# Factor rows of the attention stage read back from DRAM in two DMAs of 64 rows each

## The chip, the cores and the metric

The kernel runs on one core of one Trainium2 chip. The metric is the device time of one execution in microseconds (us). Names of the engines, as the profile writes them: PE is the matrix engine, PEld its weight loads, DVE the vector engine, ACT the scalar engine, POOL the GpSimd engine, and SP the queue that issues most DMAs. A DMA is issued by a queue (SPq, ACTq, POOLq), runs on the core's DMA engines, and counts up a semaphore when its data has landed; whoever uses the data waits for that count.

## The reference

Two decoder layers over 1024 tokens of width 1024: a short convolution with a channel mixer, then sliding-window attention with a channel mixer. The change lies in the attention of the second layer:

```python
q = rmsnorm(q, q_gain)          # per head, 16 heads of 64
k = rmsnorm(k, k_gain)
scores = einsum(q, k) / sqrt(64) + alibi        # blocks of 128 queries, window of 128
p = softmax(concat([scores, sink]))[..., :-1]
out = einsum(p, v)
return out @ w_o
```

Two kinds of factors in it go through DRAM: the inverse root mean square of each query's head, by which q is multiplied, and the inverse of each softmax sum, by which out is multiplied.

## The kernel before

Activations lie with channels on the 128 partitions and the 1024 tokens along the row. Query tile i is 128 partitions by 1024 tokens and holds two heads, 64 partitions each; there are eight tiles. Products in float32 are made of three products of rounded parts (high and low), and the large projections use a scheme of seven half-size products in place of eight, for which sums of operands were written to DRAM (`q_ops`) and are streamed back.

The attention stage is a loop of steps (`step`, line 2456) in an order written out by hand; each engine runs its instructions in that order, and a queue likewise. A step works on one block b of 128 queries of one tile i, for eight blocks of eight tiles. Its parts: scores on PE (`scores`, L2276 and L2277), row maxima on DVE (`maxima`, L2291), exponents on ACT (L2311), the turn of the block on PE (L2319), its split on ACT and DVE (L2326, L2332), the product with the values on PE (L2345, L2346) and its collection (L2363, L2364). Between them stand pieces of the projection of later tiles (`three`, L2011), whose operands come by L2526 (`q_ops`, 512 KB each, into buffers XS and WH) and whose weights come by L1948 into WR. In the last two tiles the products of the output matrix take their place (L172, weights by L128). The scores of block n+1 use a bank that the maxima of block n release, so PE's scores wait for DVE's maxima.

A factor is made in columns, one token a partition, but is needed along the rows. For query tiles 2 to 7 (`keep_q`) and for the softmax sums of all but the last pair of tiles (`divide_steps`), the way is: `rows_to_dram` (line 1713) turns the columns on PE, copies them on ACT (L1718) and stores 8 KB from ACT's queue (L1719); a step or so later `rows_from_dram` (line 1721) is issued on SP and loads the factors back with each head's row repeated on its 64 partitions; 2.5 steps after that DVE multiplies (`rows_of`, L2199, for queries into `t["raw"]`; `scale`, L2393, for out). The multiplied q is then split by ACT (L2189) and POOL (L2194), and the next tile's scores use it.

The load for queries is 128 partitions by 1024 elements, 512 KB, and there are six (the profile shows `G<-rows_q` five times and `XS<-rows_q` once). The load for softmax sums is 128 by 512, 256 KB, and there are twelve (`s<-rows_d`). They go into `t["wide"]`, which is a tile G5 or G6 (XS7 for the last), and into tile s1, of which there is one.

Each DMA of SP and ACT takes one of eight counters (DMAHW0 to DMAHW7) in turn, so that an issue also waits for the DMA that had its counter before.

Of the kernel before, what the change touches and what calls it, by code (L numbers as in the profile page):

```python
# [19 lines left out]
NB = T // P  # L20
HD = 64
# [67 lines left out]
def trunk_kernel(ctx: ExitStack, tc: tile.TileContext, xT, small, w_in, w_out, w_q, w_v, w_o, w_gu, w_dn, out):  # L89
    nc = tc.nc  # L90
# [1569 lines left out]
    def attention_layer():  # L1660
# [59 lines left out]

        def rows_from_dram(out, src, c=slice(0, D)):

            rows = src.rearrange("(h b) c -> h (b c)", h=2)[:, c]
            n = rows.shape[1]
            nc.sync.dma_start(out, rows.unsqueeze(1).to_broadcast([2, HD, n]))

        it = {}
        v = []
# [410 lines left out]
        def keep_q(i, raw_of, side=None, later=0, steps=False):  # L2139
# [34 lines left out]
            def from_dram():  # L2174
                rows_from_dram(t["wide"], t["rows"])
# [190 lines left out]
        def divide_steps(p, h, k):  # L2366
# [35 lines left out]
            def fetch():  # L2402
                it["wide"] = slot("s1", (P, HALF))
                rows_from_dram(it["wide"], rows_dram[p, h], slice(k * HALF, (k + 1) * HALF))
# [13 lines left out]
        for p in range(NK // 2):  # L2418
            for h in (0, 1):
                for k in (0, 1):  # L2420
                    *steps, sink = divide_steps(p, h, k)
                    divisions[p, h, k] = wide, rows, scale = steps
                    n = 16 * p + 16 + 6 * h + 2 * k
# [198 lines left out]
        for e in (0, 1):  # L2622
            wide, rows, scale = divisions[NK // 2 - 1, 1, e]
# [117 lines left out]
```

## Time and profile before

| | us |
|---|---|
| median of three runs | 2006.52 |
| lowest, highest run | 2000.97, 2007.32 |
| profiled execution | 2003.35 |
| its span (first to last instruction) | 2001.6 |
| PE busy in the span | 1935.8 (97%) |
| DVE busy | 1335.0 (67%) |
| ACT busy | 897.4 (45%) |
| POOL busy | 294.4 (15%) |

The profile is one execution. Its steps begin where the attention stage does, near 1040 us, and the last turned block of it is near 1311 us. Lines of waits read "engine tile line <- who ended the wait: us in total, times, longest". Lines of a timeline read "start, duration, engine, line, operation, output <- input, shape, count", and a bracket gives the idle time of the engine before it and what ended that. A line of windows gives, for each stretch, its length, the busy time of each engine with the number of its instructions, PE's granted clock as a part of full speed, the mean busy share of the DMA engines, and GB/s. Waits on an engine that is not the bound cost nothing by themselves.

### The profile page before, as it was taken

Reading aid. Unit: us, or ns where it says so; the run is one execution under the profiler, and the core shown is the slowest. Engines: PE = TensorE matmul, PEld = TensorE weight load, DVE = VectorE, ACT = ScalarE, POOL = GpSimd, SP = SyncE. Lnnn points to the kernel's source line nnn. Section 1 sums busy time; section 2 is a strip of 40 time slices with the busy share of each in tenths; the row PEclk is TensorE's granted clock in tenths of the full one; section 3 lists DMA queues with packets and bytes.
Section 4 is the critical chain, followed back from the end, with each engine's and each line's share of the span. In section 5 each row is a group of like instructions: output and inputs, shape, how many; then the busy total and the mean of one; then the engine's idle time right before and its main releaser. Section 6 shows DMA issues by size and latency. Waiting matters only on the chain.

```text
span 2001.6 us, 25275 instructions
## 1 busy us (share of the span) xinstructions
PE 1935.8 (97%) x8961; PEld 1611.1 (80%) x8961; DVE 1335.0 (67%) x2293; ACT 897.4 (45%) x1765; POOL 294.4 (15%) x367
## 2 busy tenths in 40 slices
PE   9999999999999999999997767999999999999999
PEld 8888888888888888888986656788888888888887
DVE  8898777965565566657766646788766565566553
ACT  5543555433333344544565536655433333344441
POOL 0011221011121100100143225320011111100000
PEclk9999999999999999999998878999999999999999
DMA  8787594578887559954735542141565665467663
GB/s 319 253 231 183 123 253 122 179 218 254 239 206 212 149 187 357 285 192 137 263 132 175 172 135 79 54 170 58 204 169 184 194 174 183 133 223 272 212 218 105
DMA packets 157634, 380.51 MB, mean 190 GB/s; under 512 B 15620, under 2 KB 27204, under 8 KB 157508
## 3 DMA queue, kind: packets, MB, share of 16 engines
q1 hardware_dynamic: 121732, 269.45, 39.4%
q0 software_dynamic: 35248, 109.33, 22.2%
q8 instruction: 70, 1.15, 0.2%
q14 instruction: 56, 0.46, 0.1%
q10 hardware_dynamic: 528, 0.13, 0.0%
HBM read 307.18 MB, written 149.52 MB: 228 GB/s over the span
## 4 chain that ended last, share of the span: by engine, by line
PE 89%; DMA 5%; DVE 4%; issue 1%; ACT 1%; POOL 1%; ACTq 0%; POOLq 0%; SPq 0%; DVEq 0%
PE acc L1004 16%; PE acc L1005 16%; PE acc L1007 16%; PE P L1004 9%; PE P L1005 9%; PE P L1007 9%; DMA G<-rows_q 3%; PE acc L172 2%; PE P L2011 2%; PE P L1678 1%; PE acc L176 1%; PE acc L2011 1%; PE acc L1137 1%; PE acc L1139 1%; PE acc L1138 1%
## 5 line engine op out<-in xcount | busy, mean ns | idle before, releaser
L1004 PE MATMUL acc<-XS,G 128*128 128x512 f32 x926 | 360.4, 389 | 0.0
L1005 PE MATMUL acc<-XS,G 128*128 128x512 f32 x926 | 360.2, 389 | 0.0
L1007 PE MATMUL acc<-XS,G 128*128 128x512 f32 x926 | 360.2, 389 | 0.0
L1004 PE MATMUL P<-A,G 128*128 128x512 f32 x550 | 214.1, 389 | 0.0
L1007 PE MATMUL P<-A,G 128*128 128x512 f32 x550 | 214.0, 389 | 0.0
L1005 PE MATMUL P<-A,G 128*128 128x512 f32 x550 | 214.0, 389 | 0.0
L1004 PEld LDWEIGHTS acc<-XS,G 128*128 128x128 f32 x926 | 173.8, 188 | 36.2
L1007 PEld LDWEIGHTS acc<-XS,G 128*128 128x128 f32 x926 | 173.8, 188 | 36.1
L1005 PEld LDWEIGHTS acc<-XS,G 128*128 128x128 f32 x926 | 173.8, 188 | 36.0
L1004 PE MATMUL acc<-A,G 128*128 128x512 f32 x442 | 172.1, 389 | 0.0
L1007 PE MATMUL acc<-A,G 128*128 128x512 f32 x442 | 172.0, 389 | 0.0
L1005 PE MATMUL acc<-A,G 128*128 128x512 f32 x442 | 171.9, 389 | 0.0
L938 DVE TENSOR_TENSOR G<-WR,G 128x512 fp32r<-128x512 f32 (+1 forms) x216 | 144.3, 668 | 30.5 <-ACT G L937 30.2
L938 DVE TENSOR_TENSOR G<-WL,G 128x512 fp32r<-128x512 f32 x168 | 115.1, 685 | 73.4 <-ACT G L937 73.4
L937 ACT CAST G<-WR 128x512 fp32r<-128x512 f32 (+1 forms) x216 | 130.5, 605 | 64.2 <-PE acc L1007 26.5
L937 ACT CAST G<-WH 128x512 fp32r<-128x512 f32 (+1 forms) x174 | 104.7, 601 | 82.9 <-PE acc L1007 37.9
L938 DVE TENSOR_TENSOR G<-WH,G 128x512 fp32r<-128x512 f32 (+1 forms) x174 | 115.6, 665 | 19.6 <-ACT G L937 19.6
L1339 ACT ACTIVATE G<-G 128x512 f32<-128x512 f32 x88 | 55.8, 634 | 158.9 <-DVE G L1436 153.1
L1004 PEld LDWEIGHTS P<-A,G 128*128 128x128 f32 x550 | 103.2, 188 | 21.5
L1007 PEld LDWEIGHTS P<-A,G 128*128 128x128 f32 x550 | 103.2, 188 | 21.4
L1005 PEld LDWEIGHTS P<-A,G 128*128 128x128 f32 x550 | 103.2, 188 | 21.4
L937 ACT CAST G<-WL 128x512 fp32r<-128x512 f32 x168 | 103.4, 616 | 23.9 <-DVE WL L886 12.9
(420 smaller groups left out, 3798.7 us busy)
## 6 DMA issues: line engine op xcount, KB each, us to landing
G<-h SPq DMA_DIRECT2D x70, 512.0 KB, 6.1
s<-in_w_dn SPq DMA_DIRECT2D x32, 704.0 KB, 8.7
h<-X POOLq DMA_DIRECT2D x44, 512.0 KB, 5.3
s<-s POOLq DMA_DIRECT2D x32, 704.0 KB, 7.0
WR<-s SPq DMA_DIRECT2D x79, 256.0 KB, 3.1
WR<-in_w_gu SPq DMA_DIRECT2D x36, 512.0 KB, 3.2
WH<-in_w_gu SPq DMA_DIRECT2D x36, 512.0 KB, 3.1
XS<-q_ops SPq DMA_DIRECT2D x36, 512.0 KB, 7.4
```

The source lines that it names most:

```text
L172: pe.matmul(ps.half(h), wh, xs[:, j, c], start=first and j == 0, stop=False)
L176: pe.matmul(ps.half(h), wl, xs[:, 0, c], start=False, stop=last)
L937: lambda: act.copy(out_hi, raw),
L938: lambda: lo_eng.tensor_tensor(out_lo, raw, plain(out_hi), ALU.subtract),
L1004: pe.matmul(ps, w[:, 0, c], x[:, 0, :], start=start and e == 0, stop=False, skip_group_check=True)
L1005: pe.matmul(ps, w[:, 0, c], x[:, 1, :], start=False, stop=False, skip_group_check=True)
L1007: pe.matmul(ps, w[:, 1, c], x[:, 0, :], start=False, stop=last, skip_group_check=True)
L1137: pe.matmul(ps, hi[:, kc], xs[:, 0, c], start=k == 0, stop=False, skip_group_check=True)
L1138: pe.matmul(ps, hi[:, kc], xs[:, 1, c], start=False, stop=False, skip_group_check=True)
L1139: pe.matmul(ps, lo[:, kc], xs[:, 0, c], start=False, stop=k == n_op - 1, skip_group_check=True)
L1339: state["silu"] = act.activation(x, x, AF.Silu)
L2011: pe.matmul(ps, g[:, w, c], x[:, b, :], start=begin and i == 0, stop=end and i == 2, skip_group_check=True)
```

## The change

`rows_from_dram` issues two DMAs in place of one: head 0's row to partitions 0 to 63, then head 1's row to partitions 64 to 127. Bytes, the place in the order, and everything else are as before. All 18 loads change.

```diff
         def rows_from_dram(out, src, c=slice(0, D)):
 
-            rows = src.rearrange("(h b) c -> h (b c)", h=2)[:, c]
-            n = rows.shape[1]
-            nc.sync.dma_start(out, rows.unsqueeze(1).to_broadcast([2, HD, n]))
+            for h in (0, 1):
+                row = src[h * NB : (h + 1) * NB].rearrange("b c -> (b c)")[c]
+                nc.sync.dma_start(out[h * HD : (h + 1) * HD, :], row.unsqueeze(0).to_broadcast([HD, row.shape[0]]))
```

The source of the DMA before is described as 2 rows, each repeated 64 times, of n elements; each of the two DMAs after it is described as 64 repeats of n elements.

SP's queue has 726 entries after the change and 708 before. These are its rows around the first load of query factors, before and then after; in brackets are the counts that each waits for.

```order
L2526 DMA XS_1106_7534<-q_ops 128x2x512 [waits DMAHW6_49,PE_49]
L1725 DMA G_1241_8733<-rows_q_8839 128x1x1024 [waits DMAHW3_49,Activation_49]
L2526 DMA XS_1113_7572<-q_ops 128x2x512 [waits DMAHW7_49,PE_49]
L1948 DMA WR_7842<-s_104 128x512 [waits DMAHW0_49,Pool_49]
L1948 DMA WR_7842<-s_104 128x512 [waits DMAHW1_49,Pool_49]
```

```order
L2526 DMA XS_1106_7534<-q_ops 128x2x512 [waits DMAHW6_49,PE_49]
L1725 DMA G_1241_8733<-rows_q_8839 64x1024 [waits DMAHW3_49,Activation_49]
L1725 DMA G_1241_8733<-rows_q_8839 64x1024 [waits DMAHW7_49]
L2526 DMA XS_1113_7572<-q_ops 128x2x512 [waits DMAHW0_49,PE_49]
L1948 DMA WR_7842<-s_104 128x512 [waits DMAHW1_49,Pool_49]
L1948 DMA WR_7842<-s_104 128x512 [waits DMAHW2_49,Pool_49]
```

The second half took the place and the counter of the operand load behind it, and the loads behind it in these rows moved by one counter.

On DVE no row was added. These are its rows around the multiplication that uses that load (G_1241_8733), after the change and then before it.

```order
L2364 TENSOR_TENSOR G_1218_8569<-P_1269_8948,G_1218_8569 64x2x2x64 [waits Activation_49]
L2199 TENSOR_TENSOR G_1176_8270<-G_1176_8270,G_1241_8733 128x512 [waits DMAHW7_49,DMAHW6_49]
L2291 ISA G_1187_8368,mx_8596<-P_1270_8958,cst_61 128x192 [waits PE_49]
L2291 ISA mx_8596 128x1
L2291 ISA G_1187_8368,mx_8596<-P_1270_8958,cst_61 128x192
L2291 ISA mx_8596 128x1
L2199 TENSOR_TENSOR G_1176_8270<-G_1176_8270,G_1241_8733 128x512
```

```order
L2364 TENSOR_TENSOR G_1218_8569<-P_1269_8947,G_1218_8569 64x2x2x64 [waits Activation_49]
L2199 TENSOR_TENSOR G_1176_8270<-G_1176_8270,G_1241_8733 128x512 [waits DMAHW6_49]
L2291 ISA G_1187_8368,mx_8596<-P_1270_8957,cst_61 128x192 [waits PE_49]
L2291 ISA mx_8596 128x1
L2291 ISA G_1187_8368,mx_8596<-P_1270_8957,cst_61 128x192
```

The first multiplication waits for two counters in place of one; the row maxima (L2291) stand behind it on DVE as before.

## The prediction

> **What bounds the kernel now.** I read five views in this order: the page, the waits by engine in the attention stretch, the timeline and the windows there, and the chain that ended last. Of the page, the line of PE's busy tenths (40 slices of 50 us):
>
> ```profile
> PE   9999999999999999999997767999999999999999
> ```
>
> PE sets the pace of nearly the whole program. The exception is slices 22 to 25, from 1050 to 1250 us, where it is busy to 6 or 7 tenths. That is the attention stage, the only one that calls the changed function. The next view is who waited for whom from 1040 to 1330 us, the first row of PE's, then those of DVE on factor rows; the columns are total us, times, longest.
>
> ```profile
> PE P L2276 <- DVE mx L2291: 41.4, 14, 9.0
> ```
>
> ```profile
> DVE G L2199 <- DMA G<-rows_q: 21.9, 3, 9.5
> ...
> DVE WH L2199 <- DMA G<-rows_q: 15.9, 2, 7.9
> DVE G L2393 <- DMA s<-rows_d: 5.6, 2, 3.5
> ...
> DVE XS L2199 <- DMA XS<-rows_q: 3.8, 1, 3.8
> ```
>
> PE's scores (L2276) wait for DVE's row maxima, and DVE itself waits for the factor rows: 21.9 + 15.9 + 3.8 = 41.6 us for the six tiles of queries and 5.6 us for the denominators. The timeline of the first such stop shows issue, use, and PE's first matmul after it (start, duration, and in brackets the idle time before it and what ended it).
>
> ```profile
> 1067.54 0.61 SPq L1725 DMA_DIRECT2D G<-rows_q  x1
> 1081.68 0.69 DVE L2199 TENSOR_TENSOR G<-G,G 128x512 f32<-128x512 f32 x1 [8.52 <-DMA G<-rows_q]
> 1083.35 0.53 PE L2276 MATMUL P<-A,G 128*128 128x192 f32 x1 [8.09 <-DVE mx L2291]
> ```
>
> The load takes 14.1 us from issue to use. DVE was ready for it at 1081.68 - 8.52 = 1073.16, so it has 5.6 us of cover and is 8.5 us late. Why it takes so long is in the windows: one while only such a load runs, one of full traffic, and one of a whole period of 16 steps. The last three columns are PE's granted clock, the mean busy share of the DMA engines, and GB/s.
>
> ```profile
> 1197.00:1200.00 3.00, 0.00 (x0) 0.00 (x0) 0.00 (x0) 0.00 (x0) 0.00 (x0) 0.58 0.13 53
> 1062.04:1073.16 11.12, 10.58 (x68) 8.73 (x67) 10.16 (x34) 8.18 (x30) 3.02 (x4) 1.00 0.85 279
> 1062.04:1139.73 77.69, 55.91 (x305) 47.03 (x304) 45.38 (x127) 39.51 (x124) 20.82 (x19) 0.78 0.49 158
> ```
>
> Alone, the load keeps a share of 0.13 busy. The page averages over 16 engines, so that is two of them, 26 GB/s each. Under full traffic 0.85 x 16 = 13.6 engines carry 279 GB/s, 21 each. So each of the two engines runs as fast as any; there are just two. 512 KB at 53 GB/s is 9.9 us. The source of the load has an outer dimension of 2, the heads.
>
> A third thing: what is issued behind the load suffers too. This is a piece of the chain (start, duration), a 256 KB weight load two places behind the third factor load in SP's queue.
>
> ```profile
> 1147.19 14.44 DMA WR<-s
> ```
>
> **The change, part by part.** Each of 18 loads becomes two. What it adds: 18 issues on SP. The next SP row after the first load stands for the second issue, since that issue takes its place in the queue and the counter it waited for; below it is what PE lost to late operands from 1040 to 1330 us.
>
> ```profile
> 1068.26 0.55 SPq L2526 DMA_DIRECT2D XS<-q_ops  x1
> PE acc L2011 <- DMA XS<-q_ops: 0.3, 1, 0.3
> ```
>
> The SP row came 0.72 us after the load's issue. 18 x 0.72 = 13 us of SP's time, spread over the stage; behind it stand prefetches of operands and weights. I cost it at nothing: PE lost 0.3 us to a late operand in all. Without that cover each late issue would cost at most its 0.72 us. DVE's one wait on two counters adds no instruction (the rows on DVE's order in the section on the change).
>
> What it removes: each new load has an outer dimension of 64 on both sides. If engines follow that dimension, each half goes over all 16. No row shows such a load spread wide, so I bound it by other 256 KB loads of this stretch (count, KB, median us from issue to landing):
>
> ```profile
> WR<-in_w_o SPq DMA_DIRECT2D x16, 256.0 KB, 5.5
> ...
> WR<-in_w_q SPq DMA_DIRECT2D x6, 256.0 KB, 4.0
> XS<-q_ops SPq DMA_DIRECT2D x13, 512.0 KB, 7.2
> ```
>
> (The last row is of the first period alone, 1062 to 1140 us.) With 4.0 us the second half lands 0.72 + 4.0 = 4.7 us after the first issue, 0.9 inside the 5.6 us of cover. With 5.5 us it is 0.6 late, with 7.2 us 2.3 late. I take the 0.6, rounded up to 1 us: the first two rows have the new loads' size, and I take the worse.
>
> The Trainium skill, "DMA: Bandwidth & Descriptors", section "Why a DMA increments its semaphore by 16 and not by 1", says that a DMA uses the largest number of engines up to 16 that divides the slowest dimension of both sides. The 0.13 agrees with its answer for 2; for 64 it gives 16, and then my estimate from that page's number and the 26 GB/s is an eighth of 9.9 us, 1.2 us, for the bytes, and the sum below would be 72 us, with nothing late. No run here shows that yet.
>
> What the removed wait is worth is more than the wait, as PE restarts slowly (the granted clock above is 0.58 in the stop) and ACT and POOL catch up. So I take steps, not waits. Each step of this stage turns one block of probabilities on PE (L2319); these are the starts of one period of 16 steps, two tiles of queries.
>
> ```profile
> 1062.04 0.38 PE L2319 MATMUL P<-cst,G 128*128 128x128 f32 x2
> 1065.64 0.60 PE L2319 MATMUL P<-cst,s 128*128 128x128 f32 x4
> 1067.92 0.60 PE L2319 MATMUL P<-cst,G 128*128 128x128 f32 x4
> 1070.63 0.60 PE L2319 MATMUL P<-cst,G 128*128 128x128 f32 x4
> 1073.15 0.60 PE L2319 MATMUL P<-cst,s 128*128 128x128 f32 x4
> 1085.22 1.05 PE L2319 MATMUL P<-cst,G 128*128 128x128 f32 x4
> 1090.97 0.60 PE L2319 MATMUL P<-cst,G 128*128 128x128 f32 x4
> 1098.43 0.63 PE L2319 MATMUL P<-cst,s 128*128 128x128 f32 x4
> 1101.09 0.38 PE L2319 MATMUL P<-cst,G 128*128 128x128 f32 x2
> 1103.63 0.60 PE L2319 MATMUL P<-cst,G 128*128 128x128 f32 x4
> 1105.91 0.60 PE L2319 MATMUL P<-cst,s 128*128 128x128 f32 x4
> 1111.56 0.66 PE L2319 MATMUL P<-cst,G 128*128 128x128 f32 x4 [2.86 <-ACT s L1718]
> 1124.67 1.05 PE L2319 MATMUL P<-cst,G 128*128 128x128 f32 x4
> 1129.54 0.60 PE L2319 MATMUL P<-cst,s 128*128 128x128 f32 x4
> 1132.05 0.60 PE L2319 MATMUL P<-cst,G 128*128 128x128 f32 x4
> 1135.44 0.60 PE L2319 MATMUL P<-cst,G 128*128 128x128 f32 x4
> 1139.73 0.38 PE L2319 MATMUL P<-cst,s 128*128 128x128 f32 x2
> ...
> 1218.88 0.38 PE L2319 MATMUL P<-cst,G 128*128 128x128 f32 x2
> ```
>
> First period, 77.69 us. Ten steps are untroubled: 3.60, 2.28, 2.71, 2.52, 2.66, 2.54, 2.28, 2.51, 3.39, 4.29, in sum 28.78. Six are not: 12.07 and 13.11 (the factor loads), 5.65 (a denominator), and 5.75, 7.46 and 4.87 behind the stops, 48.91 in sum. I replace the first three by 2.6 (the plain steps' size), 7.46 by 4.3 (it holds a tile's statistics, as the 4.29 does), and the other two by 3.6 (the slowest plain step): 19.3. The period saves 48.9 - 19.3 = 29.6 and becomes 48.1. The second, 1218.88 - 1139.73 = 79.15, holds the same work: 31.1. For the two tiles after it I scale by waits. The three on tile G are 21.9 with the longest 9.5 and the first 8.5, so the fifth wait is 3.9; the sixth is 3.8; together 7.7. In the first period waits of 8.5, half of 15.9, and 3.5 (the longer of those on s), 20.0 in sum, cost 29.6, or 1.48 us for each us of wait: 11.4. Sum: 72.1 us. The other end is nothing gained, or less, below.
>
> What is late next is the stream of operands. 158 GB/s x 77.69 us is 12.3 MB a period, and in 48.1 us that is 255 GB/s, near the 279 of the row under full traffic, at which PE still ran its 2.5 us steps. At 279 a period can't be under 44 us, which caps the gain: 33.7 + 35.1 and, by the same ratio (33.7 / 20.0 = 1.69), 13.0, or 82 us; 4 more if the two steps behind the last stop shrink as those of the first period do (5.75 - 3.6 each). I charge 6 us for the crowding, the 1 us for each of the six query loads; the loads of denominators are half as long and stand at nothing. So 72 - 6 = 66 us. The profiled execution took 2003.35 us (span 2001.6): **2003 - 66 = 1937 us**. It lies 3 us under the median of the runs, 2006.52; I leave that in the range.
>
> **The rivals.**
>
> *Late behind the stream.* The halves land no sooner than the 512 KB operands, 7.2 us: 0.72 + 7.2 - 5.6 = 2.3 us late of 8.5, and so 73% of 72 is saved, 53 us: 1950. At the far end the pair lands as late as its bytes take now, 9.9 us, half of the wait stays, and 2003 - 36 = 1967 is left. For it: the 255 GB/s of the stream. Against it: the extra load on two engines goes, which held up what was issued behind it (14.44 above).
>
> *Nothing gained.* The halves use as many engines between them as before, one after the other, so the second lands when the whole did: 2003, within 0.3%, which is about what a measurement of this kernel can tell from no change. For it: bytes and rows are the same. Against it: 53 GB/s is far under the 279. The Trainium skill says this in "DMA: Bandwidth & Descriptors", section "Rules for kernel authors": two transfers to disjoint partition halves serialize on the same engines, and one DMA of 128 partitions is the better. No run here shows halves; the 0.13 shows that this one DMA of 128 is not spread, which that rule takes for granted.
>
> *Slower.* The pace belongs to the row that is read, not to the shape: one DRAM row feeds 26 GB/s, as the trace shows for two rows. A half then takes 256 KB / 26 = 9.9 us, and where both halves queue on one engine the pair takes 19.8 in place of 9.9. It decides from the point where the pair needs over 14.1 us to its use. Six loads x 9.9 = 59 us more: 2062. Against it: 26 GB/s is above the 21 that an engine gets under full traffic, so the engine looks like the limit.
>
> **How the numbers follow.** Forecast 0.64, from 2003 - 86 = 1917 to 1944, midway to the next case; late behind the stream 0.27, 1944 to 1967; nothing gained 0.05; slower 0.04. The first two make faster 0.91, the others same 0.05 and slower 0.04. The range is that of the first two but for the last 4 us, which I leave out with a fifth of that case: 1917 to 1963, some 0.85.
>
> **What would show it.** In the new profile a factor load alone should show a share far above 0.13; DVE's waits on rows_q should fall from 41.6 to under 8 us; the twelve-us steps should become 2.6, and the granted clock in the period rise from 0.78 towards 1; and 256 KB loads behind the rows should land in 4 to 6 us. If the share stays at 0.13 the mechanism is wrong; if PE waits for q_ops operands, the stream is the new bound; if the span after 1330 us changes length, I have missed something.

## The result and the profile after

| | before | after |
|---|---|---|
| median of four runs, us | 2004.22 | 1956.61 |
| lowest, highest run | 2000.97, 2007.32 | 1955.13, 1958.83 |
| profiled execution, us | 2003.35 | 1958.83 |
| its span, us | 2001.6 | 1956.8 |
| last turned block (L2319) starts at | 1310.55 | 1266.14 |

The ratio is 0.9764, with an interval of 0.9742 to 0.9785: 47.6 us less by the medians. In the profiled executions it is 44.5 us, and the last turned block starts 44.4 us earlier, so the whole gain lies in the attention stage. The forecast was 66 us, 1937. The loads became faster as told; the saving was about two thirds of what was forecast.

The first line of the page that answers to those of before is that of PE's busy tenths (40 slices, now of 49 us):

```profile
PE   9999999999999999999999888999999999999999
```

Three slices of 8 are left where there were four of 6 and 7. The waits from 1030 to 1300 us (total us, times, longest) say what went and what came:

```profile
PE P L2276 <- DVE mx L2291: 10.7, 13, 1.8
...
PE P L2276 <- POOL G L2194: 5.3, 2, 2.7
...
DVE G L2199 <- DMA G<-rows_q: 2.0, 2, 1.4
```

DVE's waits for query factors fell from 41.6 us to these 2.0 and 0.4 more on tile WH; those for denominators (5.6) are gone. PE's waits for the maxima fell from 41.4 to 10.7. The row between is what to look at: PE waits for POOL's split of the new queries (L2194), 2.7 us at the longest. The same wait was there before, and it was shorter:

```profile
PE P L2276 <- POOL G L2194: 3.4, 2, 1.8
```

The first load in the timeline, its two issues in one row, then its use:

```profile
1068.40 1.12 SPq L1725 DMA_DIRECT2D G<-rows_q  x2
...
1073.80 0.69 DVE L2199 TENSOR_TENSOR G<-G,G 128x512 f32<-128x512 f32 x1 [0.58 <-DMA G<-rows_q]
```

From issue to use it takes 5.4 us where it took 14.1, and DVE is 0.58 us late where it was 8.5. The DMAs of the stage (count, KB each, median us from issue to landing) show that the loads around it gained too:

```profile
XS<-q_ops SPq DMA_DIRECT2D x28, 512.0 KB, 5.0
...
WR<-s SPq DMA_DIRECT2D x11, 256.0 KB, 5.8
G<-rows_q SPq DMA_DIRECT2D x10, 256.0 KB, 5.8
```

Before, the first two of these rows were:

```profile
XS<-q_ops SPq DMA_DIRECT2D x28, 512.0 KB, 8.3
...
WR<-s SPq DMA_DIRECT2D x9, 256.0 KB, 15.0
```

Now the steps of the first period, where about half of the missing time lies (one row a step, the start first):

```profile
1073.21 0.60 PE L2319 MATMUL P<-cst,s 128*128 128x128 f32 x4
1076.48 0.60 PE L2319 MATMUL P<-cst,G 128*128 128x128 f32 x4
1083.93 1.05 PE L2319 MATMUL P<-cst,G 128*128 128x128 f32 x4
1091.98 0.60 PE L2319 MATMUL P<-cst,s 128*128 128x128 f32 x4
...
1102.03 0.60 PE L2319 MATMUL P<-cst,G 128*128 128x128 f32 x4
1106.48 0.60 PE L2319 MATMUL P<-cst,G 128*128 128x128 f32 x4
1111.31 0.60 PE L2319 MATMUL P<-cst,s 128*128 128x128 f32 x4
1113.83 0.60 PE L2319 MATMUL P<-cst,G 128*128 128x128 f32 x4
1117.70 0.60 PE L2319 MATMUL P<-cst,G 128*128 128x128 f32 x4
1124.42 0.63 PE L2319 MATMUL P<-cst,s 128*128 128x128 f32 x2
```

The step of 12.07 us is now 3.27, that of 13.11 is 4.45. But the two steps behind the first stop, 5.75 and 7.46 before, are now 7.45 and 8.05: longer, not shorter. In the second period the steps at the same place take 6.59 and 7.50. What happens in them is in the timelines of POOL and of PE:

```profile
1075.29 1.27 POOL L2194 TENSOR_TENSOR G<-G,G 64x512 fp32r<-64x512 f32 x1 [2.72 <-ACT G L2189]
1079.39 1.27 POOL L1955 TENSOR_TENSOR WL<-WR,WL 128x512 fp32r<-128x512 f32 x1 [2.83 <-PE acc L2011]
1080.74 3.96 POOL L2194 TENSOR_TENSOR G<-G,G 64x512 fp32r<-64x512 f32 x3
```

```profile
1082.06 0.42 PE L2276 MATMUL P<-A,G 128*128 128x64 f32 x1 [2.67 <-POOL G L2194]
```

PE's next scores need two splits by POOL. The second stands in POOL's order behind a split of weights (L1955), which waits 2.83 us for PE to finish with a buffer. So PE waits for POOL, and POOL for PE. The windows (length, busy time of PE, PEld, DVE, ACT, POOL, then granted clock, DMA share, GB/s) show what follows:

```profile
1062.08:1124.42 62.34, 54.34 (x305) 45.70 (x304) 46.39 (x132) 40.34 (x127) 21.19 (x19) 0.88 0.66 207
...
1079.00:1092.00 13.00, 10.33 (x42) 9.12 (x41) 5.08 (x19) 6.49 (x21) 5.08 (x4) 0.61 0.43 138
1084.00:1092.00 8.00, 8.00 (x35) 7.47 (x34) 2.23 (x8) 2.47 (x9) 0.70 (x1) 0.51 0.39 132
1092.00:1102.00 10.00, 10.00 (x68) 8.84 (x67) 8.81 (x27) 6.58 (x23) 3.42 (x4) 1.00 0.94 270
```

After that wait PE runs 8 us without a gap at a granted clock of 0.51, through the whole of the next step. Full speed returns at 1092, with 270 GB/s of traffic.

### The profile page after: what moved, and what is told of

Same layout as the page of the kernel before. It is cut to its first block, busy times and chain, and to the rows that moved or that the text cites. A ratio compares the mean times of both kernels' runs of the same rounds, so it can differ in the third digit from the quotient of the medians.

```text
span 1956.8 us, 25325 instructions
## 1 busy us (share of the span) xinstructions
PE 1926.2 (98%) x8961; PEld 1603.0 (82%) x8961; DVE 1336.6 (68%) x2293; ACT 897.2 (46%) x1765; POOL 294.8 (15%) x367
## 4 chain that ended last, share of the span: by engine, by line
PE 91%; DVE 4%; ACT 1%; issue 1%; DMA 1%; POOL 1%; ACTq 0%; SPq 0%; POOLq 0%; DVEq 0%
PE acc L1004 16%; PE acc L1005 16%; PE acc L1007 16%; PE P L1004 9%; PE P L1005 9%; PE P L1007 9%; PE acc L172 2%; PE P L2011 2%; PE acc L2011 1%; PE P L1678 1%; PE acc L176 1%; DMA G<-rows_q 1%; PE acc L1137 1%; PE acc L1138 1%; PE acc L1139 1%
```

## The experiments

Two questions: does the gain come from the description of the source, as the prediction has it, and why was it 20 us smaller? For the second, two theories: C, that PE's wait for POOL and the half clock behind it cost the missing time; D, that the steps are held by the work of DVE and POOL itself. (The C in the expectation for the 4 x 16 repeats is another one.) All ratios are to the kernel before, on the same chip, whose medians there were 2003.1 to 2004.9.

**Two DMAs, but by columns.** The kernel before, each load cut in two along the row. There are as many issues as in the change, but each source keeps its outer dimension of 2.

```diff
-            n = rows.shape[1]
-            nc.sync.dma_start(out, rows.unsqueeze(1).to_broadcast([2, HD, n]))
+            n = rows.shape[1] // 2
+            for i in (0, 1):
+                part = rows[:, i * n : (i + 1) * n]
+                nc.sync.dma_start(out[:, i * n : (i + 1) * n], part.unsqueeze(1).to_broadcast([2, HD, n]))
```

> Each load in two DMAs, but cut by columns: both heads, half of the elements each. Theory A, the outer dimension of the description sets the number of DMA engines: it is still 2, so a lone load still shows a share of 0.13 and 53 GB/s, DVE still waits about 40 us on rows_q, and the time stays within 0.3% of before, 2004. Theory B, two DMAs in flight are what helped: waits of a few us, about 1957.

Measured 1999.13 us, ratio 0.998 (0.9967 to 0.9994). A window in which only such loads run, from 1194 us:

```profile
1194.00:1198.00 4.00, 3.54 (x12) 2.76 (x12) 0.87 (x2) 3.13 (x9) 1.07 (x1) 0.50 0.13 51
```

The share stays 0.13, the rate 51 GB/s. DVE's waits on rows_q are 16.2 + 13.9 + 4.0 = 34.1 us, 7.5 less than before. That would fit DVE using the first half sooner. The gain of two DMAs by themselves is 4.8 us here, a tenth of the change's.

**Two DMAs of 64 rows, described as 4 x 16 repeats.** The change with one more dimension in the source, same bytes, same places, same issues.

```diff
-                nc.sync.dma_start(out[h * HD : (h + 1) * HD, :], row.unsqueeze(0).to_broadcast([HD, row.shape[0]]))
+                nc.sync.dma_start(out[h * HD : (h + 1) * HD, :], row.unsqueeze(0).unsqueeze(0).to_broadcast([4, HD // 4, row.shape[0]]))
```

> The change, but each half's source is described as 4 x 16 repeats in place of 64. Theory A: four engines, a share of 0.25 and about 105 GB/s while a load is alone, 512 KB in 5 us in place of 9.9; so about 3.6 us late in place of 8.5, and 2004 less about 55% of 47 us, 1975 to 1982. Theory B: as the change, about 1957. Theory C, the row that is read sets the pace: no use of more engines, 53 GB/s or less whatever the description, 2004.

Measured 1981.77 us, 0.9889 (0.9873 to 0.9905). Its window with only such a load:

```profile
1186.00:1188.00 2.00, 0.00 (x0) 0.00 (x0) 0.80 (x2) 0.10 (x1) 0.00 (x0) 1.00 0.26 98
```

0.26 x 16 is four engines, and 98 GB/s is twice the 51. DVE's waits on rows_q are 20.7 us (13.4, 6.5 and 0.8). With the outer dimension at 2, 4 and 64 the time goes 1999, 1982, 1957. In the change itself, the load of the last query tile stands alone on SP's queue; while it moves its data the window is:

```profile
1211.00:1213.00 2.00, 2.00 (x13) 1.79 (x13) 1.50 (x6) 0.73 (x3) 0.00 (x0) 0.91 0.93 252
```

0.93 x 16 is 15 engines on the mean, so with 64 the load is spread over all or nearly all of them. As only the description differs between this kernel and the change, the number of engines is the cause.

**Query loads alone, denominator loads alone.** Six or twelve of the loads cut by heads, the rest as before. The edit of the first:

```diff
+            if c == slice(0, D):
+                for h in (0, 1):
+                    row = src[h * NB : (h + 1) * NB].rearrange("b c -> (b c)")[c]
+                    nc.sync.dma_start(out[h * HD : (h + 1) * HD, :], row.unsqueeze(0).to_broadcast([HD, row.shape[0]]))
+                return
```

The other has `!=` in place of `==`.

> Only the six loads of query factors are cut by heads; those of the denominators stay single. If the gain is worth its waits (41.6 us against 5.6 us), most of it comes here: 1960 to 1968. If the two engines that the single denominator loads still fill hold up everything behind them, less: 1970 to 1985, with DVE waits on rows_q above 8 us.

> Only the twelve loads of denominators are cut by heads. By the waits (5.6 of 47 us): 1995 to 2002, with DVE still waiting 35 us or more on rows_q. If the denominator loads held up the query loads in the two engines' queues: 1975 to 1990.

Query loads alone gave 1967.3 us, 0.9816 (0.9799 to 0.9832); denominators alone 1998.25, 0.9973 (0.9958 to 0.9988). The gains are 36.7 and 5.7 us, in sum 42.4 of the change's 47.6; the intervals don't tell whether the two help each other.

**Four DMAs of 32 rows.** Twice the issues of the change, 72 in all, each with an outer dimension of 32.

```diff
-            for h in (0, 1):
-                row = src[h * NB : (h + 1) * NB].rearrange("b c -> (b c)")[c]
-                nc.sync.dma_start(out[h * HD : (h + 1) * HD, :], row.unsqueeze(0).to_broadcast([HD, row.shape[0]]))
+            for q in range(4):
+                row = src[q // 2 * NB : (q // 2 + 1) * NB].rearrange("b c -> (b c)")[c]
+                nc.sync.dma_start(out[q * HD // 2 : (q + 1) * HD // 2, :], row.unsqueeze(0).to_broadcast([HD // 2, row.shape[0]]))
```

> The change cut once more: four DMAs of 32 rows for each load, so 36 more issues on SP, about 20 us of its time. Theory A gives an outer dimension of 32, hence all engines as with 64. If issues cost nothing, as the prediction has it: 1955 to 1960. If each load's last issue, 1.2 us later than before, makes DVE late, up to 1.2 us for each of six: 1958 to 1966, with waits on rows_q up from 2.4 to 5 us or more.

Measured 1958.1 us, 0.9766 (0.9749 to 0.9782), the same as the change. 36 more issues cost nothing that shows, so the 18 of the change don't either.

**POOL's second split one place earlier.** Now the second question. The change run again beside the next three kernels gave 1958.43 us, 0.9775 (0.9762 to 0.9789).

> The change itself, without an edit, timed beside the three below on the same chip: 1955 to 1959 by every theory.

Its profile shows what repeats: the two steps behind the first stop are 7.46 and 7.84 there, and PE's waits for POOL's split are 5.3 us again. The last step of the first period is 4.31 in place of 6.72, at a clock of 1.00. From the start of the first period to the last turned block it takes 201.3 us where the first profile took 204.1, so a difference of 3 us between two single profiles shows nothing yet.

In the next kernel the second split (L2194) is planned half a step sooner, ahead of the split of weights that blocked it.

```diff
-                (rows[1] + 1, [lambda: part_lo(0, 1)]),
+                (rows[1] + (0.5 if by_dma else 1), [lambda: part_lo(0, 1)]),
```

> The change, with POOL's second split (L2194 of the low part, head 1 of the first half) planned half a step earlier, so that on POOL it stands ahead of a weight split (L1955) and not behind it. Theory C, the steps behind the old stops stay long because PE waits 2.7 us for that split, in tiles 2 and 4, and then runs at half clock: the wait goes, the 7.5 and 8.1 us steps become about 5 and 4.3, 6 us for each of two tiles, 1943 to 1948. Theory D, those steps are long because DVE is full and its multiplications run beside POOL at 1.7 us in place of 0.7: the wait only changes its place, 1953 or more.

Measured 1948.93 us, 0.9724 (0.9708 to 0.974): 9.5 us under the change, between the two forecasts and nearer to C's. PE's waits for POOL's splits of queries are gone from its rows. Its waits for DVE's maxima rose instead, from 10.7 to 14.4 us, so a part of the wait only changed its place, as D has it. In the second period the step that took 7.50 us is 4.30. But in the first period the half clock is not gone. This is its window at the place that ran at 0.61:

```profile
1079.00:1092.00 13.00, 11.81 (x51) 10.50 (x51) 7.05 (x26) 7.54 (x23) 4.85 (x5) 0.61 0.51 162
```

The longest gap of PE ahead of it is 1.17 us there and the last one 0.84, both waits for DVE's maxima, and with two short ones PE idles 2.6 us of the 5.9 from 1075.35 to 1081.28. Its step of 8.05 is still 8.11. The wait for POOL costs time by itself, and the half clock comes without it too.

**PE kept busy in the gap.** The change, with 16 matmuls of 256 columns whose result nobody reads ahead of the first scores of tiles 2 and 4. They only keep PE from idling.

```diff
+            if b == 0 and i in (2, 4):
+                for _ in range(16):
+                    pe.matmul(ps[:, 1, :], hi[:, g, 0:P], hi[:, g, 0 : 2 * P], start=True, stop=True)
```

> The change, with 16 matmuls of 256 columns that nobody reads put ahead of the first scores of tiles 2 and 4, into the bank that those scores then overwrite; they add 2 us of PE's work where it waits 2.7. Theory C: the granted clock stays at 1.0 where it was 0.50 for ten us, and the steps of 7.5 and 8.1 us become about 6.5 and 4.5: 1946 to 1951. If the clock falls for another reason, or costs nothing: 1956 to 1961.

Measured 1951.27 us, 0.9737 (0.9724 to 0.9751), 7.2 us under the change though PE has more to do, and 0.3 us above C's stretch. The same window:

```profile
1079.00:1092.00 13.00, 11.97 (x85) 10.43 (x83) 8.43 (x27) 9.10 (x30) 7.25 (x7) 1.00 0.64 212
```

The clock stays at 1.00, and the step of 8.05 us becomes 4.29 (1083.05 to 1087.34), the 4.3 that the prediction had put for it. The step of 7.45 is 6.64, since POOL's splits come no sooner. So the half clock of that step is shown to cost 3.8 us there.

**POOL's first split on DVE.** The change, with the first of the four splits moved to DVE, so that POOL has less to do and doesn't run beside DVE's second multiplication.

```diff
-                (rows[1] + 0.5, [lambda: part_lo(0, 0)]),
+                (rows[1] + 0.5, [lambda: part_lo(0, 0, dve if by_dma else pool)]),
```

> The change, with POOL's first split of each tile (six of 1.27 us) put on DVE (about 0.7 us each). Theory D: POOL no longer runs beside the second multiplication, which falls from 1.7 to 0.7 us, and DVE is no busier than before: 1945 to 1953. Theory C: the second split comes no earlier, since it stands behind the weight split, and PE's wait stays: 1954 to 1960.

Measured 1960.21 us, 0.9784 (0.977 to 0.9799): no gain. The second split still stands behind the split of weights, PE's waits for POOL are 6.1 us, and the steps are 8.15 and 7.67. In this form D falls. But one thing it shows well. DVE multiplies each query tile in two halves, and the second half, from the change and then from this kernel, is:

```profile
1075.33 1.78 DVE L2199 TENSOR_TENSOR G<-G,G 128x512 f32<-128x512 f32 x1
```

```profile
1074.99 0.69 DVE L2199 TENSOR_TENSOR G<-G,G 128x512 f32<-128x512 f32 x1
```

With POOL's split beside it (1075.29 to 1076.56) the same instruction takes 1.78 us, without it 0.69. The Trainium skill, "SBUF — State Buffer", section "SBUF: two separate sides", says that DVE and GpSimd share a pair of ports under an exclusive lock, so that one blocks until the other's instruction ends, also for a DVE operation with two inputs in SBUF. The 1.1 us lost beside a POOL instruction of 1.27 us agrees.

**Both.** The earlier split, and 8 unread matmuls ahead of the first scores of tiles 2 to 7.

```diff
-                (rows[1] + 1, [lambda: part_lo(0, 1)]),
+                (rows[1] + (0.5 if by_dma else 1), [lambda: part_lo(0, 1)]),
...
+            if b == 0 and i > 1:
+                for _ in range(8):
+                    pe.matmul(ps[:, 1, :], hi[:, g, 0:P], hi[:, g, 0 : 2 * P], start=True, stop=True)
```

> early_lo, with 8 matmuls of 256 columns that nobody reads ahead of the first scores of tiles 2 to 7. Theory C, what early_lo left over is the half clock in the first period (0.61 from 1079 to 1092, a step of 8.1 us that was 4.3 in the run fill): the clock stays up, 4 us less than early_lo, 1942 to 1947. Theory D, DVE is the bound there by now and PE's clock no longer matters: 1948 to 1953, as early_lo or a little more.

Measured 1949.49 us, 0.9721 (0.9706 to 0.9735). C had expected 1942 to 1947, D 1948 to 1953, so the time is D's here. The first period, from 1062.41 us:

```profile
1062.41:1118.07 55.66, 49.51 (x322) 41.27 (x320) 44.35 (x127) 39.45 (x124) 21.59 (x19) 1.00 0.73 224
```

The clock is 1.00 throughout, and the period is 2.5 us shorter than the 58.15 of the earlier split alone. The last turned block starts at 1255.97 in place of 1259.17, so this profiled execution kept the 3 us. The medians don't show them: 3 us is 0.15%, and each interval is 0.3% wide; and two profiles of the change alone differed by 2.8 us in this stage. So the filling is neither shown to help on top of the earlier split nor to harm. The earlier split alone, which adds no work, is the version that beats both kernels: 1948.9 us.

## Why the prediction was right or wrong

- **What bounds the kernel, two engines per load**: right, and shown. 2, 4 and 64 in the outer dimension gave shares of 0.13, 0.26 and 0.93. The Trainium skill's rule in "DMA: Bandwidth & Descriptors", section "Why a DMA increments its semaphore by 16 and not by 1", gives 2 and 4 engines for the first two, as measured. The Trainium skill's advice against halves, on the same page in "Rules for kernel authors", was the rival "nothing gained"; it doesn't hold for this load, whose one DMA wasn't spread.
- **Issues on SP cost nothing**: right, by the four DMAs of 32 rows. That DVE's two-counter wait adds no instruction was wrong by 21 ns: the trace has an event wait of that length ahead of each of the six first multiplications.
- **Landing**: 4.7 to 6.2 us after the first issue was expected, 5.4 came. The first lateness of 0.6 is 0.58. The 6 us charged for crowding were too many; DVE's waits add up to 2.4.
- **What the removed wait is worth**: here the prediction failed, in the size of a term. It replaced six steps of a period by plain ones and got 48.1 us; the periods are 62.34 and 59.70 (1124.42 to 1184.12). The savings are 15.4 and 19.5 where 29.6 and 31.1 stood; behind the periods 9.7 where 11.4 stood. That is 27.7 us too much, less the 6 charged: 21.6, the whole difference from 66.1 to 44.5.
- **Which replacements failed**: 2.6 for the stops held nearly (3.27; 4.45 for the second). 3.6 for the step behind the first stop became 7.45, and 4.3 for the one with the statistics 8.05: 7.6 us of the first period's 14.3. The last step, taken over at 4.29, became 6.72 at a clock of 0.61, 2.4 more; but in the second profile of the same kernel it was 4.31, so these 2.4 belong to one execution. The remaining 4.2 lie in steps with the clock at 1.00. The prediction put the 5.75 and 7.46 down to the stop. Part of the 5.75 was another wait, already in the trace of before, and 2.67 after:

```profile
1089.96 0.30 PE L2276 MATMUL P<-A,G 128*128 128x64 f32 x1 [1.56 <-POOL G L2194]
```

- **A floor that the prediction didn't work out**: at a full clock (the window of the last experiment) PE is still busy 49.51 us in a period. Sixteen of its matmuls are the filling, 2.2 us at the 0.136 us each takes in the timeline of the kernel with 16, so about 47 are its own. DVE had 45.38 us of work in the first period by the prediction's own row. A period of 48.1 would have both busy over 94% of the time while each waits for the other at every step. So even without the half clock the period came to 55.66. How much of the 7.6 us between is the filling itself (2.2 at most), DVE's second multiplication or the order of the hand-over wasn't tried.
- **Next limit, the operand stream**: wrong. The period runs at 207 GB/s, and no wait of PE for a `q_ops` load is left among its waits.
- **The rivals**: 1956.6 lies in the stretch of "late behind the stream", but not for that reason, since DVE's waits on rows_q nearly vanished. The forecast's own stretch, 1917 to 1944, was missed; the range held because it took in most of this other case, which is luck. "Nothing gained" and "slower" fell with the share and the landing.
- **What would show it**: the waits on rows_q under 8 us, and 256 KB loads behind the rows in 4 to 6 us, came as told, and so did a share far above 0.13 (0.93). The twelve-us steps fell to 3.3 and 4.5, not 2.6, and the clock of the period rose from 0.78 to 0.88 only, which is where the missing time shows.

## What to carry to other kernels

A DMA that keeps a share of 0.13 busy while it runs alone is on two engines, and the description of its source may be all that holds it there; one more issue is a cheap price. Before pricing the end of a stall, add up each engine's work in that stretch at a full clock, as a floor, and look in the steps behind it for a second, smaller wait that the stall hides. A step that was long behind a stall can't be counted as short without it until what made it long is known.

## What the runs showed of the hardware

- PE was busy for 8.00 of 8.00 us and its granted clock stayed at 0.51 all that time; in these 8 us stand 16 matmuls of only two columns (L1678). The Trainium skill, "TensorE: Matmul & The Clock Gate", section "What's actually happening", has full speed return after a busy window of about 3.4 us. The measured 8 us differ from that, if busy means what the profile counts. In the trace of before, two busy stretches at half clock without such matmuls were back at full speed 4.3 us (from 1162.5) and 6.0 us (from 1123.2) after PE had started. It would fit that the narrow matmuls don't count; no run tried it.
- The length of a wait alone doesn't tell whether the clock falls. Behind the same wait of 1.09 us, in the last step of the first period, it fell in one profile of the change (0.61 over the step) and stayed at 1.00 in the other. Unread matmuls put behind a gap of 0.75 us kept it at 1.00 in the first period.
- A load on two engines holds up what is issued behind it on the queue: the 256 KB loads from `s` landed 15.0 us after their issue before, 5.8 after; with the query loads alone spread it was 5.3, with the denominators alone 12.7.
- A DVE multiplication of 128x512 takes 0.69 us alone and 1.78 beside a POOL subtraction of 1.27.
